# m kept in DRAM as two parts, split where it is made, and six early pairs of the second feed-forward, each split ahead of the puts

## The chip, the cores and the metric

One core of a Trainium2 chip runs the whole kernel. The metric is the device time of one execution in microseconds. Before the change it is 2270.53 us, the median of three runs (2268.02 to 2271.82). The engines are named as the profile names them: PE (TensorE, matmuls), PEld (its weight loads), DVE (VectorE), ACT (ScalarE), POOL (GpSimd) and SP (the sync engine, which issues loads).

## The reference

One layer of a trunk on 1024 tokens of width 1024: a half-step feed-forward, a token mixing of two branches (retention and neighbourhood attention), and a second half-step feed-forward, each with RMS norms before and after. What matters here is the end of the mixing and the start of the second feed-forward:

```python
merged = jax.nn.sigmoid(g_ret) * y_ret + jax.nn.sigmoid(g_na) * y_na
return merged @ w_out
...
x = x + _rms_norm(m, mix_post_norm[l])
h = _swiglu(_rms_norm(x, ffn2_pre_norm[l]), ffn2_w_in[l], ffn2_w_out[l])
x = x + 0.5 * _rms_norm(h, ffn2_post_norm[l])
```

## The kernel before

Every matmul operand is a float32 that is **split** into two parts of a rounded type, h and l with h + l the value: `split` (L56) casts h on ACT and subtracts on DVE to get l. `mm3` (L86) then makes one product of three matmuls, h·h, h·l and l·h. `piece` (L75) splits 512 columns of a weight into `wh` and `wl`, of which there are eight buffers each.

**Making m** (L1453 to L1479). `merged`, here called m, is made feature by feature: eight tiles of 128 features x 1024 tokens in the groups 0 to 2, 3 to 5 and 6 to 7. For each tile 48 matmuls make `y_ret`; DVE multiplies the two banks by the gate (`sr`, loaded into the tile `m`, L1477) and adds the other branch (tile `z`, L1478), and POOL's queue stores the tile to DRAM (L1479). The tiles `m` and `z` have four buffers each.

**Mix-out** (`out_proj`, L137, called at L1508). `merged @ w_out` runs over token blocks of 128 in three groups: blocks 0 to 2, 3 to 5, 6 and 7. In a group the loop goes over the eight k, the feature tiles of m; in the last three k the blocks are finished one after another. `stream` (L842) brings the left side: SP loads the k's slice of m (`graw`, two buffers), and `split` makes `gh` and `gl` (three buffers each). `wload` (L1490) brings the weights, which stay for all groups. When a block is finished, `Ep` (L210) makes its norm and residual, stores x2 and starts the norm for the feed-forward; its last step, a closure in the list `left`, turns the block by eight transposes on PE (`flip`, L122) and hands it to `Winograd.put` (L264).

**The puts.** The second feed-forward's first matmul is done by a scheme with seven products in place of eight (Winograd). Its left operands are a11 and a12 from blocks 0 to 3, and a22, s1, s2, s3 and s4, for which blocks 4 to 7 are needed too. The put of a block from 4 to 7 is eleven operations of DVE and seven of ACT.

**Pairs** (L409). One pair is the gate tile and the up tile of 128 features. `run` (L494) makes its products: a11, s2, a12, s3, s1, a22, s4, 12 matmuls each. Products a11 and a12 don't need blocks 4 to 7, so `lead` (L454) makes them early, between mix-out and the last puts: before the change for four pairs. Three pairs stay in PSUM (pairs 0, 1, 2, "held"), and one (pair 3, "saved") is made first and copied to SBUF, in pieces of 256 columns in buffers of `gh` and `gl`, through `save` (L1512). The list `between` holds the closures that mix-out left over (the flips of blocks 6 and 7, then the last steps of their puts); one is taken after each early pair. After that, `ffn_in` (L539) runs all 22 pairs; the first four are "begun" and lack two products. In `run`, `t2` is the operand of product s2, and L510, L511, L521 and L530 are the four subtractions on weights; `LeftFactors` (L562) splits and stores what a pair has made for the next matmul.

The order on each engine is the scheduler's; each engine executes its own queue in order. PE's work is cut into stages whose windows the prediction names: making m, mix-out, the lead (mix-out's end to the first product s2), the begun pairs, and the rest.

Of the kernel before, what the change touches and what calls it, by code (L numbers as in the profile page):

```python
# [1 line left out]

# [8 lines left out]
F32 = mybir.dt.float32  # L11
F32R = mybir.dt.float32r
# [6 lines left out]
P = 128  # L19
D = 1024  # L20
S = 1024
KT = D // P
TT = S // P
DFF = 2816
FT = DFF // P
# [13 lines left out]
class Core:  # L39
# [16 lines left out]
    def split(self, h, l, src, scale=None, eng=None):  # L56

        nc = self.nc
        hf = h.bitcast(F32)
        if scale is None:  # L60
            self.done = [nc.scalar.copy(h, src).ins,  # L61
                         (eng or nc.vector).tensor_tensor(l, src, hf, ALU.subtract).ins]  # L62
        else:
            nc.scalar.activation(h, src, AF.Copy, scale=scale)
            nc.vector.scalar_tensor_tensor(l, src, scale, hf, op0=ALU.mult, op1=ALU.subtract)
# [336 lines left out]
def xslice(xop):  # L402
    def f(k, h):
        s = slice(h * 512, (h + 1) * 512)
        return xop[0][k // 4][:, k % 4, s], xop[1][k // 4][:, k % 4, s]
    return f


class Pairs:  # L409
# [41 lines left out]
                               k == 0, k == 3)  # L451
                    yield

    def lead(self, save=None, between=(), on_pool=(), abreast=1, extra=0):  # L454


        n = self.held + self.saved
        tiles = [i for i in (*range(self.held, n), *range(self.held), *range(n, n + extra)) if i not in self.begun]
        while tiles:
            group, tiles, abreast = tiles[:abreast], tiles[abreast:], 1  # L460
            for i in group:
                if i not in self.fetched:
                    self.fetch(i)
            g = [self.fetched.pop(i) for i in group]
            eng = self.c.nc.gpsimd if group[0] in on_pool else None
            tag = ("ps", 6) if group[0] < n else ("pt", 2)
            ps = [self.products("a11", [self.ready.pop(i, w[:, :512]) for i, w in zip(group, g)], eng, tag),
                  self.products("a12", [w[:, 512:] for w in g], eng, tag)]
            if between:
                f = between.pop(0)()  # L470
                if f is not None:
                    between.append(f)
            for i, *pair in zip(group, *ps):
                if self.held <= i < n:
                    sb = [save(), save()]
                    for a, b in zip(sb, pair):
                        for p, s in self.pieces(a):
                            self.c.nc.scalar.copy(p, b[:, s])
                    pair = sb
                self.begun[i] = pair  # L480
# [358 lines left out]
    return flips  # L839


def stream(c, pool, src):  # L842

    def lhs(k, toks):
        n = len(toks) * P
        p0 = toks[0] * P
        raw = pool.tile([P, 384], F32, tag="graw", name="graw", bufs=2)
        h = pool.tile([P, 384], F32R, tag="gh", name="gh", bufs=3)
        l = pool.tile([P, 384], F32R, tag="gl", name="gl", bufs=3)
        c.nc.sync.dma_start(raw[:, :n], src(k)[:, p0:p0 + n])  # L850
        c.split(h[:, :n], l[:, :n], raw[:, :n])
        return {t: (h[:, j * P:(j + 1) * P], l[:, j * P:(j + 1) * P]) for j, t in enumerate(toks)}
    return lhs

# [344 lines left out]
def trunk_layer(ctx: ExitStack, tc, x, xt, g1a, w1i, w1o, g1b, gma, wmt, wnv, wrv, logits, dtab, rope, bias,  # L1199
# [7 lines left out]
    c = Core(tc, const, wpool, psum, dram)  # L1207
# [3 lines left out]
    def dt(name, shape):  # L1211
        return dram.tile(shape, F32, name=name)

    gl = [{n: dram.tile([FT // 2, P, 1024], F32, name=f"g{i}{n}") for n in Winograd.NAMES} for i in range(2)]
    x1, x2 = dt("x1", [S, D]), dt("x2", [S, D])
    d = {
        "a21": dt("a21", [P, 4, 512]),
        "nq": dt("nq", [NHP, P, S]), "nk": dt("nk", [NHP, P, S]), "nv": dt("nv", [16, 64, 512]), "nvg": dt("nvg", [4, 4, P, 512]),
        "no": dt("no", [NHP, P, S]), "rq": dt("rq", [RH, P, S]), "rk": dt("rk", [RH, P, S]),
        "rv": dt("rv", [TT, P, D]), "rg": dt("rg", [8, P, S]), "ry": dt("ry", [8, P, S]),  # L1220
        "sr": dt("sr", [8, P, S]), "sn": dt("sn", [8, P, S]), "z": dt("z", [8, P, S]), "m": dt("m", [8, P, S]),
    }

    def rows(a):
        return lambda t: a[t * P:(t + 1) * P, :]

    right, left = ExitStack(), ExitStack()

    def pool(stack, name, side="left"):
        return stack.enter_context(tc.tile_pool(name=name, bufs=1, side=side, reuse_waits="tile"))  # L1230
# [3 lines left out]
    early = pool(right, "early", "right")  # L1234
    wx = Winograd(c, apool, early, None, order=("s4", "a22", "s3", "a12", "s1", "s2", "a11"))
    g0 = pool(left, "gl10")
    with tc.tile_pool(name="fin1", bufs=1, reuse_waits="tile") as fp:
        def lead():
            return early.tile([P, 512], F32, tag="lead", name="lead", bufs=6)
# [5 lines left out]
        fin = Pairs(c, wx, [(w1i[i], w1i[FT + i]) for i in LeftFactors.order], 3, 3)  # L1245
# [4 lines left out]
        for _ in steps:  # L1250
# [8 lines left out]
    wx = Winograd(c, (x0pool, x1pool, spool), None, (4, 4, 2, 8, 8, 8, 8), d["a21"])  # L1259
# [5 lines left out]
    q = [p.tile([P, 4, 512], F32, tag="x", name="q", bufs=n) for p, n in ((ep, 2), (ep, 2), (spool, 8), (spool, 8))]  # L1265
    ahead = {}
    fo = Epilogue(c, ep, g1b, gma, rows(x), rows(x1), wx.put)
    rest = ffn_out(c, [[b11, b12], [b21, b22]], q, Blocks(c, (g0, *[g1] * 6)), w1o, gl[0], fo, tail,
                   {n: (lambda j=j: ahead.update({j: c.load_w(wnv[j])})) for j, n in enumerate((65, 66))})
# [63 lines left out]
    with tc.tile_pool(name="pa", bufs=1, reuse_waits="tile") as pa:  # L1333
# [12 lines left out]
        for i, (_, _, f, g, fn) in enumerate(jobs):  # L1346
# [18 lines left out]
            if i == 2:  # L1365
                x1pool = pool(x1_stack, "x1b", "right")
                a21[:] = [x1pool.tile([P, 4, 512], F32R, name=f"a21{q}") for q in "hl"]
                for k in range(2):
                    raw = c.raw(d["a21"][:, 2 * k:2 * k + 2].rearrange("p k t -> p (k t)"))
# [78 lines left out]
    gs = pool(g_stack, "gs2", "right")  # L1448
    ro = pool(y_stack, "ro")
    for k in range(KT):  # L1450
        raw = c.raw(d["ry"][k])
        c.split(yop[0][k // 4][:, k % 4], yop[1][k // 4][:, k % 4], raw)
    for i0 in (0, 3, 6):  # L1453
        tiles = range(i0, min(i0 + 3, 8))
        m, z, w, banks = {}, {}, {}, {}
        for i in tiles:
            w[i] = wr.pop(i) if i in wr else c.load_w(wro[i])
            banks[i] = [c.bank() for _ in range(2)]
            for q, name, src in ((m, "m", "sr"), (z, "z", "z")):
                q[i] = ro.tile([P, S], F32, tag=name, name=name, bufs=4)  # L1460
                nc.sync.dma_start(q[i], d[src][i])

        def one(i, k):
            ks = slice((k % 4) * P, (k % 4 + 1) * P)
            for h in range(2):
                c.mm3(banks[i][h], [p[:, ks] for p in w[i][k // 4]], xslice(yop)(k, h), k == 0, k == KT - 1)


        for k in range(KT if i0 == 0 else 0):
            for i in tiles:  # L1470
                one(i, k)
        for i in tiles:
            for k in range(KT if i0 > 0 else 0):
                one(i, k)
            for h in range(2):
                hs = slice(h * 512, (h + 1) * 512)
                nc.vector.tensor_tensor(m[i][:, hs], banks[i][h], m[i][:, hs], ALU.mult)  # L1477
                nc.vector.tensor_tensor(m[i][:, hs], m[i][:, hs], z[i][:, hs], ALU.add)  # L1478
            c.store(d["m"][i], m[i])  # L1479
    y_stack.close()  # L1480
    m_stack.close()

    a_stack, wm_stack = ExitStack(), ExitStack()
    apool = pool(a_stack, "a2", "right")
    wm = pool(wm_stack, "wm", "right")
    cmb = pool(left, "cmb2")
    wx = Winograd(c, apool, cmb, None, order=("s1", "s3", "a12", "s2", "a11"))
    held = {}

# [15 lines left out]

    with tc.tile_pool(name="ep2", bufs=1, reuse_waits="tile") as ep:
        ks = tuple(range(KT))
        rest = c.out_proj(KT, stream(c, gs, lambda k: d["m"][k]), wload,  # L1508
                          Ep(c, ep, gmb, g2a, False, rows(x1), rows(x2), wx.put), (ks, ks, ks[4:] + ks[:4]), lags={4: 11})
        fin = Pairs(c, wx, [(w2i[i], w2i[FT + i]) for i in LeftFactors.order], 3, 1)  # L1510

        def save():  # L1512
            return [gs.tile([P, 384], F32, tag=n, name=n, bufs=3)[:, :256] for n in ("gh", "gl")]

        rest.insert(0, lambda: None)
        fin.lead(save, rest)
        for f in rest:
            f()

# [7 lines left out]
    w = [w2.tile([P, 4, 512], F32, name=f"w{i}") for i in range(12)]  # L1527
    tiles = [[[w[n] for n in m] for m in q] for q in (((11, 10, 9), (8, 7, 6)), ((2, 1, 0), (5, 4, 3)))]
    with tc.tile_pool(name="out2", bufs=1, reuse_waits="tile") as op:
        q = [op.tile([P, 4, 512], F32, tag="q", name="q", bufs=4) for _ in range(4)]  # L1530
# [82 lines left out]
```

## Time and profile before

| what | value |
|---|---|
| median of 3 runs | 2270.53 us |
| the profiled execution, whole | 2266.95 us |
| its span, first to last instruction | 2265.2 us |
| mean granted clock of PE | 0.992 |
| moved by DMA | 439.91 MB, mean 194 GB/s |
| mix-out's first and last split of m's slices | 1484.1 and 1610.4 us |

The profile's page gives shares over the whole span. The stages are read from windows (busy time of each engine in a stretch), the causes from the wait views (who waited for whom), and single steps from the timeline, where a row is the start, the duration, the engine, line, operation, output and inputs, the count, and in brackets the idle time before it and what ended it. Matmul rows overlap: a matmul of 512 columns is shown as 0.39 us, and the next starts 0.227 us after it.

### The profile page before, as it was taken

To read this page: it belongs to the slowest core of one execution; us is meant where nothing else is said; L and a number is where in the kernel's file an instruction comes from. 1 tells how busy PE (TensorE), PEld (TensorE's weight loads), DVE (VectorE), ACT (ScalarE), POOL (GpSimd) and SP (SyncE) were. 2 spreads that over 40 slices of the span, in tenths; PEclk is the share of its full clock that TensorE was granted. 3 is DMA by queue.
4 is the path that set the end of the run, shared out by engine and by line. 5 is a ranking of instruction groups with operands and counts; after the bars stand their busy time and mean duration, and the time that the engine had idled before them with its cause. 6 is when DMAs were issued, how large, how long until landed. Compare 5 with 4: busy or idle time off the path is not lost. (4 is left out here: it accounts for less than half of the span.)

```text
span 2265.2 us, 30039 instructions
## 1 busy us (share of the span) xinstructions
PE 2204.2 (97%) x10232; PEld 1830.1 (81%) x10232; DVE 1641.4 (72%) x2928; ACT 984.5 (43%) x2054; POOL 575.8 (25%) x747
## 2 busy tenths in 40 slices
PE   6899999999998999999999999999999999999998
PEld 5688888888786887878888888887778888888886
DVE  7898878765558757769885678544998787876444
ACT  5444434332344322248885676323644343433232
POOL 1121212168521122311101222101112121215942
PEclk9999999999999999999999999999999999999999
DMA  6354434597545554557655466764345444449765
GB/s 251 134 181 150 177 130 170 187 387 294 199 174 174 180 173 134 145 181 241 217 173 174 151 230 233 259 232 144 117 156 188 149 161 147 154 157 378 283 225 180
DMA packets 150345, 439.91 MB, mean 194 GB/s; under 512 B 19056, under 2 KB 46832, under 8 KB 148080
## 3 DMA queue, kind: packets, MB, share of 16 engines
q1 hardware_dynamic: 108912, 305.84, 39.4%
q0 software_dynamic: 41280, 132.15, 16.2%
q8 instruction: 81, 1.33, 0.2%
q14 instruction: 72, 0.59, 0.1%
HBM read 297.41 MB, written 144.70 MB: 195 GB/s over the span
## 5 line engine op out<-in xcount | busy, mean ns | idle before, releaser
L62 DVE TENSOR_TENSOR wl<-wraw,wh 128x512 fp32r<-128x512 f32 x472 | 317.1, 689 | 66.3 <-ACT wh L61 66.0
L61 ACT CAST wh<-wraw 128x512 fp32r<-128x512 f32 x476 | 274.2, 618 | 169.2 <-PE ps L89 69.2
L88 PE MATMUL ps<-wh,g 128*128 128x512 f32 x484 | 188.8, 390 | 0.0
L89 PE MATMUL ps<-wl,g 128*128 128x512 f32 x484 | 188.7, 390 | 0.0
L90 PE MATMUL ps<-wh,g 128*128 128x512 f32 x484 | 188.5, 390 | 0.0
L552 ACT ACTIVATE c<-c 128x512 f32<-128x512 f32 x88 | 55.5, 632 | 208.0 <-DVE c L517 107.6
L62 DVE TENSOR_TENSOR wl<-w,wh 128x512 fp32r<-128x512 f32 x77 | 77.9, 1031 | 86.3 <-ACT wh L61 86.1
L62 DVE TENSOR_TENSOR wl<-x,wh 128x512 fp32r<-128x512 f32 x77 | 78.4, 1035 | 78.3 <-ACT wh L61 77.1
L61 ACT CAST wh<-t 128x512 fp32r<-128x512 f32 x58 | 36.0, 621 | 195.0 <-DVE t L511 194.9
L88 PE MATMUL ps<-a11h,wh 128*128 128x512 f32 x276 | 111.5, 404 | 7.9 <-ACT wh L61 7.9
L90 PE MATMUL ps<-a11h,wl 128*128 128x512 f32 x276 | 109.7, 398 | 7.3 <-DVE wl L62 7.2
L90 PE MATMUL ps<-a12h,wl 128*128 128x512 f32 x276 | 108.7, 394 | 3.4 <-DVE wl L62 3.4
L88 PE MATMUL ps<-a12h,wh 128*128 128x512 f32 x276 | 109.7, 397 | 0.5 <-ACT wh L61 0.3
L89 PE MATMUL ps<-a11l,wh 128*128 128x512 f32 x276 | 109.8, 398 | 0.1
L90 PE MATMUL ps<-a22h,wl 128*128 128x512 f32 x280 | 109.3, 390 | 0.6 <-DVE wl L62 0.6
L88 PE MATMUL ps<-a22h,wh 128*128 128x512 f32 x280 | 109.8, 392 | 0.0
L89 PE MATMUL ps<-a22l,wh 128*128 128x512 f32 x280 | 109.2, 390 | 0.0
L89 PE MATMUL ps<-a12l,wh 128*128 128x512 f32 x276 | 108.2, 392 | 0.0
L89 PEld LDWEIGHTS ps<-wl,g 128*128 128x128 f32 x484 | 90.9, 188 | 19.1 <-DVE wl L62 0.5
L90 PEld LDWEIGHTS ps<-wh,g 128*128 128x128 f32 x484 | 90.9, 188 | 18.8
L88 PEld LDWEIGHTS ps<-wh,g 128*128 128x128 f32 x484 | 90.9, 188 | 18.7
L88 PE MATMUL ps<-s2h,wh 128*128 128x512 f32 x232 | 91.9, 396 | 6.6 <-ACT wh L61 6.5
(438 smaller groups left out, 6411.4 us busy)
## 6 DMA issues: line engine op xcount, KB each, us to landing
wraw<-in_dram SPq DMA_DIRECT2D x202, 512.0 KB, 4.5
g<-g0s SPq DMA_DIRECT2D x44, 512.0 KB, 4.2
g<-g1s SPq DMA_DIRECT2D x44, 512.0 KB, 4.9
g<-g0a SPq DMA_DIRECT2D x33, 512.0 KB, 3.3
g<-g1a SPq DMA_DIRECT2D x33, 512.0 KB, 4.5
g0s<-gth POOLq DMA_DIRECT2D x44, 256.0 KB, 4.7
g0s<-cmb POOLq DMA_DIRECT2D x44, 256.0 KB, 3.7
g1s<-gth POOLq DMA_DIRECT2D x44, 256.0 KB, 4.6
```

The costliest lines, as they stand in the source:

```text
L61: self.done = [nc.scalar.copy(h, src).ins, (eng or nc.vector).tensor_tensor(l, src, hf, ALU.subtract).ins]
L62: (eng or nc.vector).tensor_tensor(l, src, hf, ALU.subtract).ins]
L88: mm(ps, a[0], b[0], start=start, stop=False)
L89: mm(ps, a[0], b[1], start=False, stop=False)
L90: mm(ps, a[1], b[0], start=False, stop=stop)
L552: nc.scalar.activation(gate[j], gate[j], AF.Silu)
```

## The change

In making m, each tile is split there: ACT casts h into the tile `z`, DVE leaves l in the tile `m`, and both are stored, so the DRAM tensor m has two parts. `stream` then loads the two parts straight into the operands: two loads of a slice per k and no split. Its eight buffers of 128x512 are six in the pool `gs` and two in a new pool `gx`, the latter for every fourth k.

Six pairs are begun early instead of four: pairs 3, 4 and 5 are saved, each product as one copy of 512 columns in a buffer of the stream, then 0, 1 and 2 are held. After the products of an early pair, and before the closure from `between`, the weights of the next early pair are split (`split` in `lead`). `between` starts with a closure that does nothing, then block 6's flip, another that does nothing, block 7's flip, and so on; before, only one stood at the front.

```diff
-    def lead(self, save=None, between=(), on_pool=(), abreast=1, extra=0):
+    def lead(self, save=None, between=(), on_pool=(), abreast=1, extra=0, early=False):
+        def split(i):
+            if i not in self.fetched:
+                self.fetch(i)
+            w = self.fetched[i]
+            self.ready[i] = self.c.piece(w[:, :512])
+            self.fetched[i] = [None, self.c.piece(w[:, 512:])]
...
-            ps = [self.products("a11", [self.ready.pop(i, w[:, :512]) for i, w in zip(group, g)], eng, tag),
-                  self.products("a12", [w[:, 512:] for w in g], eng, tag)]
+            ps = [self.products("a11", [self.ready.pop(i) if i in self.ready else w[:, :512] for i, w in zip(group, g)],
+                                eng, tag),
+                  self.products("a12", [w[1] if isinstance(w, list) else w[:, 512:] for w in g], eng, tag)]
+            if early and tiles:
+                split(tiles[0])
             if between:
...
-def stream(c, pool, src):
+def stream(c, pools, src):
+    n0 = itertools.count()
     def lhs(k, toks):
...
-        raw = pool.tile([P, 384], F32, tag="graw", name="graw", bufs=2)
-        h = pool.tile([P, 384], F32R, tag="gh", name="gh", bufs=3)
-        l = pool.tile([P, 384], F32R, tag="gl", name="gl", bufs=3)
-        c.nc.sync.dma_start(raw[:, :n], src(k)[:, p0:p0 + n])
-        c.split(h[:, :n], l[:, :n], raw[:, :n])
+        last = next(n0) % 4 == 3
+        h, l = (pools[last].tile([P, 512], F32, tag="g", name="g", bufs=2 if last else 6) for _ in range(2))
+        for q, a in enumerate((h, l)):
+            c.nc.sync.dma_start(a[:, :n], src(k, q)[:, p0:p0 + n])
+        h, l = h.bitcast(F32R), l.bitcast(F32R)
...
-            c.store(d["m"][i], m[i])
+            c.split(z[i].bitcast(F32R), m[i].bitcast(F32R), m[i])
+            for q, a in enumerate((z[i], m[i])):
+                c.store(d["m"][i][q], a)
...
-        fin = Pairs(c, wx, [(w2i[i], w2i[FT + i]) for i in LeftFactors.order], 3, 1)
+        fin = Pairs(c, wx, [(w2i[i], w2i[FT + i]) for i in LeftFactors.order], 3, 3)
         def save():
-            return [gs.tile([P, 384], F32, tag=n, name=n, bufs=3)[:, :256] for n in ("gh", "gl")]
-        rest.insert(0, lambda: None)
-        fin.lead(save, rest)
+            return gs.tile([P, 512], F32, tag="g", name="g", bufs=6)
+        rest[1:1] = rest[:0] = [lambda: None]
+        fin.lead(save, rest, early=True)
```

What this does to the order of the engines shows at two places. The line numbers of the changed kernel are 1 to 12 higher.

The first place is DVE near the end of the lead, where block 7's put begins: `wl` is a split of an early pair's weight; `cmb`, `a22l` and `s1l` to `s4l` belong to the puts of blocks 6 and 7. Before, from the sum of block 7's L283 on:

```order
L283 TENSOR_TENSOR cmb<-cmb,a11l 128x512
L293 TENSOR_TENSOR cmb<-a12h,cmb 128x512
L62 TENSOR_TENSOR a22l<-pt,a22h 128x4x128
L294 TENSOR_TENSOR cmb<-cmb,a12l 128x512
L288 TENSOR_TENSOR cmb<-pt,cmb 128x512
L62 TENSOR_TENSOR s3l<-cmb,s3h 128x4x128
L62 TENSOR_TENSOR wl<-wraw,wh 128x512
L290 TENSOR_TENSOR cmb<-pt,cmb 128x512
L62 TENSOR_TENSOR s1l<-cmb,s1h 128x4x128
L62 TENSOR_TENSOR s4l<-cmb,s4h 128x4x128
L62 TENSOR_TENSOR s2l<-cmb,s2h 128x4x128
```

Now:

```order
L63 TENSOR_TENSOR wl<-wraw,wh 128x512
L63 TENSOR_TENSOR s2l<-cmb,s2h 128x4x128
L63 TENSOR_TENSOR wl<-wraw,wh 128x512
L294 TENSOR_TENSOR cmb<-a12h,cmb 128x512
L63 TENSOR_TENSOR wl<-wraw,wh 128x512
L295 TENSOR_TENSOR cmb<-cmb,a12l 128x512
L520 TENSOR_TENSOR wraw<-wraw 128x512
L283 TENSOR_TENSOR cmb<-a11h,cmb 128x512
L63 TENSOR_TENSOR a22l<-pt,a22h 128x4x128
L284 TENSOR_TENSOR cmb<-cmb,a11l 128x512
L289 TENSOR_TENSOR cmb<-pt,cmb 128x512
```

The last weight splits of the early pairs, before in the midst of block 7's put, now stand ahead of its first step (L283 in the changed kernel), among the steps of block 6's.

The second place is DVE in the begun pairs. `t_16351` is t2 of pair 3, the last that was begun before; L535 is the last add of pair 2. Before:

```order
L510 TENSOR_TENSOR wraw<-wraw 128x512
L517 TENSOR_TENSOR c_16344<-gh,gt 128x256
L532 TENSOR_TENSOR c_16199<-ps,c_16199 128x512
L511 TENSOR_TENSOR t_16351<-wraw 128x512
L517 TENSOR_TENSOR c_16344<-gl,gt 128x256
L554 TENSOR_TENSOR gt<-c_16199,gt 128x512
L62 TENSOR_TENSOR wl<-t_16351,wh 128x512
L535 TENSOR_TENSOR gt<-ps,gt 128x512
```

Now the last begun pair is pair 5, its t2 is `t_16667`, and L545 is the last add of pair 4 (L610 are splits of `LeftFactors`, L564 its gate times up):

```order
L542 TENSOR_TENSOR c_16515<-ps,c_16515 128x512
L610 TENSOR_TENSOR cmb<-cmb,gth 128x512
L520 TENSOR_TENSOR wraw<-wraw 128x512
L564 TENSOR_TENSOR gt<-c_16515,gt 128x512
L521 TENSOR_TENSOR t_16667<-wraw 128x512
L545 TENSOR_TENSOR gt<-ps,gt 128x512
L527 TENSOR_TENSOR c_16660<-g,gt 128x512
L564 TENSOR_TENSOR gt<-c_16514,gt 128x512
L63 TENSOR_TENSOR wl<-t_16667,wh 128x512
```

The split of t2 moved from ahead of the last add of the pair before it to behind that add. From the split of pair 3's t2 (`t_16406` in the changed kernel) to that of pair 5's, this one included, DVE has 47 operations.

More of the change, by code (lines that the diff above doesn't have):

```diff
@@ L1 @@
+import itertools
 from contextlib import ExitStack, nullcontext
@@ L1220, in trunk_layer @@
         "rv": dt("rv", [TT, P, D]), "rg": dt("rg", [8, P, S]), "ry": dt("ry", [8, P, S]),
-        "sr": dt("sr", [8, P, S]), "sn": dt("sn", [8, P, S]), "z": dt("z", [8, P, S]), "m": dt("m", [8, P, S]),
+        "sr": dt("sr", [8, P, S]), "sn": dt("sn", [8, P, S]), "z": dt("z", [8, P, S]), "m": dt("m", [8, 2, P, S]),
     }
@@ L1485, in trunk_layer @@
     wm = pool(wm_stack, "wm", "right")
-    cmb = pool(left, "cmb2")
+    cmb, gx = pool(left, "cmb2"), pool(left, "gx")
     wx = Winograd(c, apool, cmb, None, order=("s1", "s3", "a12", "s2", "a11"))
@@ L1507, in trunk_layer @@
         ks = tuple(range(KT))
-        rest = c.out_proj(KT, stream(c, gs, lambda k: d["m"][k]), wload,
+        rest = c.out_proj(KT, stream(c, (gs, gx), lambda k, q: d["m"][k][q]), wload,
                           Ep(c, ep, gmb, g2a, False, rows(x1), rows(x2), wx.put), (ks, ks, ks[4:] + ks[:4]), lags={4: 11})
-        fin = Pairs(c, wx, [(w2i[i], w2i[FT + i]) for i in LeftFactors.order], 3, 1)
+        fin = Pairs(c, wx, [(w2i[i], w2i[FT + i]) for i in LeftFactors.order], 3, 3)
         def save():
-            return [gs.tile([P, 384], F32, tag=n, name=n, bufs=3)[:, :256] for n in ("gh", "gl")]
-        rest.insert(0, lambda: None)
-        fin.lead(save, rest)
+            return gs.tile([P, 512], F32, tag="g", name="g", bufs=6)
+        rest[1:1] = rest[:0] = [lambda: None]
+        fin.lead(save, rest, early=True)
         for f in rest:
```

## The prediction

> **What bounds the kernel now.** First the page (engine totals), then the windows by stage. Columns of a window: length, busy us and instructions of PE, PEld, DVE, ACT and POOL, granted clock, DMA share, GB/s.
>
> ```profile
> PE 2204.2 (97%) x10232; PEld 1830.1 (81%) x10232; DVE 1641.4 (72%) x2928; ACT 984.5 (43%) x2054; POOL 575.8 (25%) x747
> ...
> 1433.00:1520.00 87.00, 87.00 (x385) 72.08 (x385) 40.35 (x58) 17.83 (x26) 5.40 (x10) 1.00 0.74 270
> 1520.00:1616.00 96.00, 94.50 (x436) 76.81 (x435) 58.79 (x107) 42.49 (x105) 11.06 (x19) 1.00 0.41 144
> 1616.00:1650.00 34.00, 28.31 (x122) 21.79 (x121) 32.64 (x57) 18.98 (x41) 4.61 (x6) 0.95 0.27 93
> 1650.00:1705.00 55.00, 54.89 (x242) 44.80 (x241) 52.93 (x89) 23.59 (x44) 8.65 (x16) 1.00 0.46 163
> 1705.00:2250.00 545.00, 545.00 (x2405) 451.34 (x2404) 381.89 (x570) 196.36 (x355) 185.96 (x218) 1.00 0.56 205
> ```
>
> TensorE is the bound, and from 1705 to 2250 it has no gap at all: whatever it gains or loses before comes out at the end one for one. The five rows are the stage that makes m, mix-out, the lead, the begun pairs, and the rest. TensorE idles 1.5 us in mix-out and 5.7 us in the lead, where VectorE is busy 32.64 of 34 us. The wait views of TensorE for these two stretches (us, times, longest) name the releasers:
>
> ```profile
> PE pt L127 <- DVE tmp L118: 0.5, 1, 0.5
> PE pt L127 <- DVE a12l L62: 0.4, 1, 0.4
> PE ps L90 <- DVE gl L62: 0.3, 1, 0.3
> PE ps L88 <- DVE tmp L225: 0.2, 1, 0.2
> ```
>
> ```profile
> PE ps L90 <- DVE wl L62: 4.8, 3, 3.4
> PE ps L88 <- ACT wh L61: 0.8, 1, 0.8
> ```
>
> All of it is VectorE and its partner ScalarE. The change leaves TensorE's matmuls as many as before and moves some, so the forecast is this idle time removed, less idle time that it adds.
>
> **Making m.** Eight splits of 128x1024 come in; the nearest rows are the same two operations on the same size, in this stage, on `ry`:
>
> ```profile
> L61 ACT CAST xy<-wraw x8: 1031/1048/1056, 1431.0 to 1446.5; 128x1024 fp32r<-128x1024 f32 x8
> L62 DVE TENSOR_TENSOR xy<-wraw,xy x8: 1214/1220/1226, 1432.9 to 1447.6; 128x1024 fp32r<-128x1024 f32 x8
> ```
>
> So 8 x 1.05 = 8.4 us of ScalarE and 8 x 1.22 = 9.8 us of VectorE, in 87 us of which they are busy 17.8 and 40.4; TensorE waits for neither. What this delays is behind it: `z` and `m` of tile i are now free only when both stores have landed, and tile i+4 loads into them. The DMA rows (KB each, median us to landing):
>
> ```profile
> z<-z SPq DMA_DIRECT2D x8, 512.0 KB, 7.8
> m<-m POOLq DMA_DIRECT2D x8, 512.0 KB, 4.9
> ...
> graw<-m SPq DMA_DIRECT2D x16, 192.0 KB, 3.3
> ```
>
> ```profile
> 1466.27 0.54 POOL L68 DMA_DIRECT2D m<-m  x1 [29.49 <-DVE m L1478]
> ```
>
> The second fence is GpSimd's first store of m in the timeline, at 1466.3. Now one cast comes ahead of it: the store of tile 0's `z` goes at about 1467.3, lands 4.9 later, and z of tile 4 is there 7.8 after that: 1480. VectorE needs it when tile 4's matmuls end, 240 matmuls of 0.227 us after the stage's start at 1434: 1488. I put **0**; the bounds are 0 and, if each landing took twice as long, 5 us. The added bytes are 4 MB out and 4 MB in; at the 270 GB/s of the first row that is 30 us of transfer laid into 183 us with DMA shares of 0.74 and 0.41.
>
> **Mix-out.** 24 splits go, on both engines:
>
> ```profile
> L61 ACT CAST gh<-graw x24: 397/514/516, 1484.1 to 1608.7; 128x384 fp32r<-128x384 f32 x16, 128x256 fp32r<-128x256 f32 x8
> L62 DVE TENSOR_TENSOR gl<-graw,gh x24: 415/551/559, 1484.7 to 1610.4; 128x384 fp32r<-128x384 f32 x16, 128x256 fp32r<-128x256 f32 x8
> ```
>
> That is 16 x 0.55 + 8 x 0.42 = 12.2 us of VectorE. They stood in front of the epilogues for which TensorE waited:
>
> ```profile
> 1559.12 0.56 DVE L62 TENSOR_TENSOR gl<-graw,gh 128x384 fp32r<-128x384 f32 x1 [0.98 <-ACT gh L61]
> ...
> 1560.22 1.41 DVE L118 SCALAR_TENSOR_TENSOR tmp<-epx,rstd,gpre 128x512 f32<-128x512 f32 x2
> ...
> 1601.02 0.39 PE L88 MATMUL ps<-wmh,gh 128*128 128x512 f32 x1
> 1601.75 0.51 PE L90 MATMUL ps<-wmh,gl 128*128 128x512 f32 x1 [0.34 <-DVE gl L62]
> ```
>
> VectorE sat 0.98 us for `gh` and then did `gl` ahead of L118; without them L118 is over 1 us earlier, more than the 0.5 us wait. A pause costs more than its idle time: 1601.02 to 1601.75 is 0.73 where 0.23 would do. The four waits cost about 3 us so counted. I take **-2.0** (bounds -3 and 0), as the wait for the bank that `a12l` frees may stay in part.
>
> The price is on the sync queue: each k takes two loads. A k-step of three blocks is 18 matmuls, 4.1 us, and a buffer pair is free about 6.8 us ahead of its use at the tightest (the eighth k of a group, in its last three). 3.3 us to landing, and some 0.4 more for the second issue, fit: **0**. Landings of twice that would stall each group once for about half a microsecond, so the bounds are 0 and 2 us.
>
> **The lead.** TensorE's rows (start, us):
>
> ```profile
> 1616.64 0.39 PE L88 MATMUL ps<-a11h,wh 128*128 128x512 f32 x1
> 1616.87 0.39 PE L89 MATMUL ps<-a11l,wh 128*128 128x512 f32 x1
> ...
> 1636.37 0.50 PE L90 MATMUL ps<-a11h,wl 128*128 128x512 f32 x1 [1.05 <-DVE wl L62]
> ...
> 1642.98 0.50 PE L90 MATMUL ps<-a12h,wl 128*128 128x512 f32 x1 [3.38 <-DVE wl L62]
> ...
> 1646.36 0.63 PE L90 MATMUL ps<-a12h,wl 128*128 128x512 f32 x1
> 1647.84 0.50 PE L88 MATMUL ps<-s2h,wh 128*128 128x512 f32 x1 [0.85 <-ACT wh L61]
> 1648.18 0.40 PE L89 MATMUL ps<-s2l,wh 128*128 128x512 f32 x1
> 1648.99 0.50 PE L90 MATMUL ps<-s2h,wl 128*128 128x512 f32 x1 [0.41 <-DVE wl L62]
> ```
>
> From 1616.64 to 1647.84 are 31.2 us for 96 matmuls (x 0.227 = 21.8) and 16 transposes (steps around them: 2.0 us); 7.4 are lost, and 0.8 more at the start of `s2`: **8.2 us**. One part is a slow clock: 0.63 instead of 0.39 us for eight matmuls after the long wait. Why the wait is there:
>
> ```profile
> 1617.33 0.21 DVE L220 TENSOR_SCALAR ss<-ss 128x1 f32<-128x1 f32 x1
> ...
> 1641.64 0.68 DVE L62 TENSOR_TENSOR s3l<-cmb,s3h 128x512 fp32r<-128x512 f32 x1
> 1642.24 0.69 DVE L62 TENSOR_TENSOR wl<-wraw,wh 128x512 fp32r<-128x512 f32 x1
> ...
> 1644.64 0.69 DVE L62 TENSOR_TENSOR s2l<-cmb,s2h 128x512 fp32r<-128x512 f32 x1
> ```
>
> The split of the last early pair stood between the steps of block 7's put. In the new order (first place above) it stands ahead of that put. And there are 144 matmuls: `s2` is reached at 1616.6 + 144 x 0.227 + 1.8 for two flips = 1651.1, in the old time. VectorE steps by 0.60 us (1641.64 to 1642.24). From block 6's epilogue (1617.33) to block 7's last first-hand split `s2l` (1644.64, done at 1645.2) it never waits for TensorE in this trace; in the new order this stretch has six operations more (three weight splits, three of the first pair), and one more to the split of the first pair's t2: 1645.2 + 7 x 0.60 = 1649.4, where TensorE wants it at the third matmul of `s2`, 1651.6. Block 7's first put step is then due 12 operations earlier, at 1642.2, and its transposes end at 1616.6 + 96 x 0.227 + 1.8 = 1640.2. So **-8.2**, with 2.2 us to spare. ScalarE gets some 5 us more (four casts, and six saves of whole banks where there were four of half ones) in a stretch where it is busy 19 of 34 us: 0.
>
> **The begun pairs.** A begun pair is five products, 60 matmuls, 13.6 us of TensorE; a full one has seven, 19.0 us. VectorE's share is 23.5 operations per pair on average (18 of its own, 11 per two pairs for the factors of the second product), 14.1 us. Already the fourth begun pair comes too late (VectorE's split of its t2, and TensorE's `s2`):
>
> ```profile
> 1689.51 0.69 DVE L62 TENSOR_TENSOR wl<-t,wh 128x512 fp32r<-128x512 f32 x1
> ```
>
> ```profile
> 1689.47 0.44 PE L88 MATMUL ps<-s2h,wh 128*128 128x512 f32 x1
> ...
> 1690.25 0.50 PE L90 MATMUL ps<-s2h,wl 128*128 128x512 f32 x1
> ```
>
> The third matmul of `s2`, due 0.45 us after the first, is 0.3 us late. Now two more begun pairs follow: the order has 47 VectorE operations after pair 3's t2 split up to pair 5's (second place above), 28.3 us, against 27.2 us of TensorE: 1.1 later; and the split now stands behind the last add of the pair before, which waits for that pair's last product: 0.6 more. Together **+2.0** at pair 5 (bounds 0 and 5: nothing if ScalarE's and VectorE's order leaves slack, twice as much if waits for a buffer's store fall in). The Trainium skill (TensorE: Matmul & The Clock Gate, "What's actually happening") lets the clock halve after an idle window of about 3.4 us; the trace agrees, with slow matmuls after 3.38 us idle and none after 1.05 or 0.85. By that rule 2 us stays without a slow clock, and a wait above 3.4 would cost some 1.4 us on top.
>
> **Sum.** 0 - 2.0 - 8.2 + 2.0 = -8.2 us. The profiled execution took 2266.95 us, so it would take 2258.7. The median of the runs is 3.6 above it, and I predict against the median: **2262.3**.
>
> **Rivals.** (1) The whole idle time goes, the begun pairs cost nothing: -11, 2259.5. For it: in the row 1650 to 1705 four begun pairs cost TensorE only 0.1 us of idle time. Against it: the count of 47 operations. (2) VectorE stays the bound in the lead or the pairs, waits move there, and only some 3 us are left: 2267.5. For it: 32.64 of 34 us busy. Against it: 12 us of work leave it just ahead. It decides once the put of block 7 starts over 2.2 us later than I count. (3) The change does not do what it says: TensorE reaches `s2` later but waits there as long as before, 2270.5. Against it: the long wait was for a weight split, not for the put. (4) Slower: the two loads of a k land one after the other. From the row that is 2 x 3.3 = 6.6 us per k-step against 4.1 in mix-out's first two groups: 16 x 2.5 = +40 us, less the gain: 2302; it decides from 4.1 us per pair of loads. Against it: in the stage before, the DMA share reaches 0.74 with 270 GB/s, and 512 KB in 4.9 or 7.8 us each would be 107 or 67 GB/s one after the other, so transfers overlap. The Trainium skill (DMA: Bandwidth & Descriptors, "Anatomy of one DMA") fits a transfer, though for the GpSimd path, as 2.0 us plus its bytes at 436 GB/s: two of 192 KB in a row would be, as an estimate, 2 x 2.45 = 4.9 us, and the loss 16 x 0.8 = 13 us. Here the trace differs: one such load took 3.3 us to landing from the sync queue.
>
> **Chances.** Forecast (-6 to -10) 0.60, (1) 0.10, (2) 0.15, (3) 0.08, (4) or any like it 0.07. Range: 2257 (all idle time gone, and the 2 us by which runs scatter) to 2270 (nearly nothing left). 0.2% is 4.5 us, about what a measurement of this kernel tells from no change: faster holds the forecast, (1) and half of (2), 0.77; same 0.16; slower 0.07.
>
> **What would show it.** In the changed profile: no wait of TensorE for `wl` between the end of mix-out and `s2`, and no slow clock there; `s2` some 34.5 us after the lead's first matmul; a TensorE wait of about 2 us for `wl` at the sixth pair's `s2`; mix-out's idle time under 0.7 us; no TensorE wait for a load of `m`. It would be wrong if VectorE reaches block 7's put after about 1644 in the old time, or if stream loads take over 6.8 us.

## The result, and the profile after

| | before | changed |
|---|---|---|
| median of 5 runs (range), us | 2268.02 (2267.3 to 2271.82) | 2259.97 (2256.05 to 2262.78) |
| span of the profiled execution, us | 2265.2 | 2258.2 |
| ratio of the runs | 1 | 0.9956, 95% interval 0.9944 to 0.9967 |

The changed kernel is faster, by 8.05 us between the medians; the ratio, taken over all runs, says 10 us, with an interval of 7.5 to 12.7. That is 0.4%, small but clear of the scatter. First the page's engine totals and the windows by stage, with the columns of the prediction's (length, busy us and instructions of PE, PEld, DVE, ACT, POOL, granted clock, DMA share, GB/s):

```profile
PE 2201.1 (97%) x10232; PEld 1828.9 (81%) x10232; DVE 1638.7 (73%) x2911; ACT 984.6 (44%) x2039; POOL 581.0 (26%) x755
```

```profile
1433.00:1520.00 87.00, 87.00 (x386) 72.05 (x385) 46.59 (x62) 22.57 (x29) 8.79 (x16) 1.00 0.84 312
1520.00:1614.00 94.00, 93.20 (x433) 76.69 (x432) 50.77 (x89) 34.51 (x85) 11.16 (x20) 1.00 0.59 199
1614.00:1650.00 36.00, 36.00 (x169) 29.96 (x168) 34.64 (x60) 23.98 (x49) 4.60 (x6) 1.00 0.29 102
1650.00:1733.00 83.00, 80.86 (x347) 65.78 (x346) 79.12 (x130) 33.47 (x60) 16.24 (x30) 0.98 0.52 184
1733.00:2240.00 507.00, 507.00 (x2238) 419.73 (x2237) 350.45 (x520) 182.54 (x329) 176.40 (x203) 1.00 0.58 208
```

Making m is full as before. Mix-out has 0.80 us of idle TensorE left, and the lead none at all. New is a hole of 2.1 us, with the clock at 0.98, in the begun pairs. From 1733 to 2240 there is no gap again, so all that was gained ahead of it reaches the end. The wait views of TensorE (us, times, longest), first mix-out, then the begun pairs; the lead's has no row.

```profile
PE ps L89 <- DVE tmp L226: 0.4, 1, 0.4
PE pt L128 <- DVE a11l L63: 0.3, 1, 0.3
```

```profile
PE ps L89 <- ACT wh L62: 1.2, 1, 1.2
PE ps L91 <- DVE wl L63: 1.0, 1, 1.0
```

The table counts TensorE's stages from first matmul to first matmul in the timelines (us). "Over" is the time above 0.227 us a matmul; the lead has 1.8 us on top for its flips, as in the prediction. The last stage is the first s2 and the 479 matmuls behind it, 108.6 us without a pause. The experiments stand in it too, told below.

| kernel | making m | mix-out | lead: early pairs, us, over | 480 matmuls, over |
|---|---|---|---|---|
| before | 87.04 | 95.64 | 4, 31.20, 7.6 | 1.4 |
| changed | 87.04 | 94.15 | 6, 34.46, 0.0 | 4.6 |
| e1_split_only | 87.05 | 94.06 | 4, 30.16, 6.6 | 3.5 |
| e2_six_only | 87.04 | 96.30 | 6, 35.97, 1.5 | 6.4 |
| e3_six_late | 87.04 | 94.06 | 6, 34.46, 0.0 | 3.0 |
| e4_pair6 | 87.04 | 94.15 | 6, 34.45, 0.0 | 0.9 |
| e5_tt_pool | 87.04 | 94.07 | 6, 34.45, 0.0 | 4.1 |
| e6_five | 87.04 | 94.13 | 5, 31.98, 3.0 | 2.9 |
| e7_double_load | 87.04 | 111.71 | 6, 34.45, 0.0 | 4.6 |
| e8_pair6_again | 87.04 | 94.05 | 6, 34.44, 0.0 | 1.3 |
| e9_double_aside | 87.04 | 94.14 | 6, 34.47, 0.0 | 4.6 |
| e10_same | 87.04 | 94.08 | 6, 34.45, 0.0 | 3.0 |

From before to changed that is 0 - 1.5 - 7.6 + 3.2 = -5.9 us. The stage that makes m also began 1.0 us earlier (1432.95 instead of 1433.96); this start lies between 1430.9 and 1440.6 in the twelve profiles and follows no edit. Together -6.9, and the spans differ by 7.0.

### The profile page after: what moved, and what is told of

It is laid out like the page before. It is cut to its first block, busy times and chain, and to the rows that moved or that the text cites. A ratio compares the mean times of both kernels' runs of the same rounds, so it can differ in the third digit from the quotient of the medians.

```text
span 2258.2 us, 30072 instructions
## 1 busy us (share of the span) xinstructions
PE 2201.1 (97%) x10232; PEld 1828.9 (81%) x10232; DVE 1638.7 (73%) x2911; ACT 984.6 (44%) x2039; POOL 581.0 (26%) x755
## 5 line engine op out<-in xcount | busy, mean ns | idle before, releaser
L89 PE MATMUL ps<-wh,g 128*128 128x512 f32 x548 | 214.2, 391 | 0.4 <-DVE tmp L226 0.4
L90 PE MATMUL ps<-wl,g 128*128 128x512 f32 x548 | 213.6, 390 | 0.0
L91 PE MATMUL ps<-wh,g 128*128 128x512 f32 x548 | 213.3, 389 | 0.0
L89 PEld LDWEIGHTS ps<-wh,g 128*128 128x128 f32 x548 | 102.9, 188 | 21.8 <-DVE tmp L226 0.7
L90 PEld LDWEIGHTS ps<-wl,g 128*128 128x128 f32 x548 | 102.9, 188 | 21.5 <-DVE wl L63 0.5
L91 PEld LDWEIGHTS ps<-wh,g 128*128 128x128 f32 x548 | 102.9, 188 | 21.4
```

The source lines that it names most:

```text
L89: mm(ps, a[0], b[0], start=start, stop=False)
L90: mm(ps, a[0], b[1], start=False, stop=False)
L91: mm(ps, a[1], b[0], start=False, stop=stop)
```

## The experiments

All are measured against the kernel before, run beside them on the same chip (three chips; the medians of the kernel before are 2268.16, 2269.57 and 2268.99 us), so ratios compare better than times. Diffs are against the changed kernel, unless said otherwise. A theory and a rival stand in each expectation.

**e1_split_only**: m in two parts, but four early pairs as before.

```diff
-        fin = Pairs(c, wx, [(w2i[i], w2i[FT + i]) for i in LeftFactors.order], 3, 3)
+        fin = Pairs(c, wx, [(w2i[i], w2i[FT + i]) for i in LeftFactors.order], 3, 1)
...
-        rest[1:1] = rest[:0] = [lambda: None]
-        fin.lead(save, rest, early=True)
+        rest.insert(0, lambda: None)
+        fin.lead(save, rest)
```

> Edit: the changed kernel with four early pairs in the old order; only m stays split in DRAM. Theory (two separate gains): mix-out loses about 1.5 us of TensorE's waits as in the changed kernel, the lead keeps its wait of 3 to 4 us for a weight split and its 8 us of loss, the last begun pair costs 0.4 us; time 1 to 2 us under the kernel before. Rival (the lead was late because VectorE came into it with a backlog from the 24 splits): the waits in the lead shrink to under 3 us in all and the time comes 5 to 7 us under the kernel before.

2267.15 us, ratio 0.9998 (0.9988 to 1.0007): no gain that can be told from the scatter. Mix-out has its 1.6 us, but the lead's wait is whole, in one piece at s2. TensorE's waits in the lead:

```profile
PE ps L89 <- ACT wh L62: 5.1, 1, 5.1
PE pt L128 <- ACT cmb L280: 0.7, 1, 0.7
PE ps L91 <- DVE wl L63: 0.5, 1, 0.5
```

So the 12 us of VectorE work that left mix-out don't free the lead by themselves, and the rival falls. That rests on the stages; the total also has the 2.1 us that the last stage lost, most of it (1.6) in eight slow matmuls behind the long wait.

**e2_six_only**: the kernel before with six early pairs split ahead of the puts, m in one part and split in mix-out (the saves go to other free buffers).

> Edit: the kernel before, with m as one part and 24 splits in mix-out, but six early pairs, each split ahead of the puts; the saves lie in pieces in the buffers of the stream. Theory: the lead has no wait over 0.3 us and s2 comes about 34.5 us after its first matmul, mix-out keeps its 1.5 us of idle time, pair 5 has the waits of the changed kernel (4 us of loss); time 4 to 5 us under the kernel before. Rival (the split in DRAM is what frees the lead): waits of 3 us or more remain in the lead, time within 2 us of the kernel before.

2263.81 us, ratio 0.9976 (0.9965 to 0.9988). Of the changed kernel's gain it has about half. One wait for a weight split is left in the lead, where the theory had none over 0.3 us:

```profile
PE ps L90 <- DVE wl L62: 1.1, 1, 1.1
```

Mix-out is 2.1 us longer than in the changed kernel, the lead 1.5, the begun pairs 1.8; the pauses at pair 5's s2 are 2.00 and 0.94 us, with slow matmuls behind them. With e1: the early pairs fill most of the lead's wait, and the split of m, worth nothing that shows alone, is worth some 4 us beside them (by the medians; part of it is the slow clock, told at the end).

**e3_six_late**: six early pairs, without the split ahead of the closures.

```diff
-        fin.lead(save, rest, early=True)
+        fin.lead(save, rest)
```

> Edit: the changed kernel, but the weights of an early pair are not split ahead of the puts; the six pairs and their places stay. Theory (the place of the splits matters by itself): VectorE does the last weight splits among the steps of block 7's put, and TensorE waits in the lead 2 to 5 us for them; time 2 to 5 us over the changed kernel. Rival (the two more pairs alone fill the wait): no wait over 0.5 us in the lead, time as the changed kernel's.

2259.83 us, ratio 0.996 (0.9949 to 0.9972), and no wait in the lead. The scheduler brings every engine's instructions into the same order as in the changed kernel, so the place of `split` in the code changed nothing, and the theory's claim for it fell. The run serves as a repeat of the changed kernel.

**e4_pair6**: six early pairs, but 0 to 4 and 6 instead of 0 to 5, so that one pair with all seven products stands ahead of the last begun one.

```diff
         tiles = [i for i in (*range(self.held, n), *range(self.held), *range(n, n + extra)) if i not in self.begun]
+        if early:
+            tiles[2] = 6
...
-            tag = ("ps", 6) if group[0] < n else ("pt", 2)
+            tag = ("ps", 6) if group[0] < n or early else ("pt", 2)
...
-                if self.held <= i < n:
+                if self.held <= i < n or early and i == 6:
```

> Edit: the changed kernel, but the early pairs are 0 to 4 and 6 in place of 5; nothing else. Theory (pair 5's s2 comes too early for VectorE, as five products are all that its predecessor gives it, and the work for the second product's factors falls there): a full pair 5 starts with a product that needs no subtraction, the waits at its s2 (1.2 and 1.0 us) and the slow matmuls after them go, and nothing as long takes their place; TensorE loses under 1 us between 1650 and 1800, time 3 to 4 us under the changed kernel. Rival (VectorE's backlog only moves on): a wait of 1.5 us or more at s2 of pair 6 or 7, time as the changed kernel's.

2257.12 us, ratio 0.9949 (0.9934 to 0.9965). The wait view of TensorE for the begun pairs (1650 to 1735), and the window that showed the hole:

```profile
PE ps L89 <- ACT wh L62: 0.3, 1, 0.3
```

```profile
1650.00:1733.00 83.00, 82.75 (x364) 67.67 (x363) 79.20 (x130) 36.04 (x64) 16.17 (x30) 1.00 0.50 181
```

VectorE is as busy as in the changed kernel (79.20 and 79.12 us), TensorE 1.9 us more: the work is the same, and a pair of 84 matmuls ahead of the last t2 gives it time. The pauses belong to too many short pairs in a row.

**e5_tt_pool**: the sums and differences of `LeftFactors` of the first six pairs on GpSimd.

```diff
-            return lambda: self.traced.append(c.nc.vector.tensor_tensor(*a).ins)
+            eng = c.nc.gpsimd if i < self.on_pool else c.nc.vector
+            return lambda: self.traced.append(eng.tensor_tensor(*a).ins)
...
-        tail = ffn_in(c, fin, fp, LeftFactors(c, cmb, fp, gl[1]))
+        tail = ffn_in(c, fin, fp, LeftFactors(c, cmb, fp, gl[1], 6))
```

> The changed kernel, but the sums and differences of LeftFactors (L589) of the first six pairs run on GpSimd instead of VectorE. Theory: in the begun pairs VectorE never pauses, and its count of operations alone sets when pair 5's t2 is split; four operations of 0.60 us fewer between pair 3's and pair 5's split bring that split 2.4 us earlier, so of its 2.5 us of lateness at most 0.5 is left, no slow matmuls follow, and the stretch of 480 matmuls after the first s2 falls from 113.2 to about 110: time about 2257. Rival: the order is held by a chain (the subtraction for t2 waits for what stands behind the last add of pair 4, or GpSimd's operations, about 1.5 us each, delay VectorE's splits behind them in its queue): then both waits at pair 5's s2 stay over 0.8 us each and the time stays at 2260 or rises.

2259.37 us, ratio 0.9962 (0.995 to 0.9975): no gain over the changed kernel. From pair 3's t2 split (1692.49) to pair 5's (1721.34) VectorE took 28.85 us, against 28.99 in the changed kernel. It had 40 operations there instead of 47, as three more (L527, L542, L564) fell outside; the 4.2 us so saved were given back at two places. At the first, an operation took 1.78 us instead of 0.68 (1696.76, 1.1 more). VectorE's and GpSimd's rows of the timeline at the second:

```profile
1713.62 0.69 DVE L612 TENSOR_TENSOR gt<-gt,gth 128x512 fp32r<-128x512 f32 x1 [2.08 <-POOL cmb L591]
1714.23 1.78 DVE L612 TENSOR_TENSOR cmb<-cmb,gth 128x512 fp32r<-128x512 f32 x1
```

```profile
1712.30 1.29 POOL L591 TENSOR_TENSOR cmb<-gt,cmb 128x512 f32<-128x512 f32 x1
...
1714.11 1.35 POOL L591 TENSOR_TENSOR cmb<-gt,cmb 128x512 f32<-128x512 f32 x1
```

A split that overwrites `gt` waited 2.08 us until GpSimd had read it, and the next one took 1.78 us instead of 0.69. TensorE still waits 0.96 us at pair 5's s2, and 0.97 us at its s3 in place of the 1.18 at s2. GpSimd's operations holding up VectorE is the rival's second half. So the run doesn't test whether the count of operations decides: VectorE was as late with fewer.

**e6_five**: five early pairs, two saved (`..., 3, 2)` in place of `..., 3, 3)`).

> The changed kernel with five early pairs (two saved) instead of six. Theory: the lead is a race of TensorE's 24 matmuls per early pair against VectorE's put of blocks 6 and 7. With 120 matmuls TensorE is at s2 120 x 0.227 + 1.8 = 29.0 us after the lead's start, its third matmul 29.45; VectorE's split of the first t2 ended 33.1 us after that start with six pairs, and three operations of 0.60 us fewer make 31.3: waits of about 1.9 us at the first s2 (and up to 1.6 us of slow matmuls), where four early pairs waited 5.1 and six none. At the last begun pair less than 1 us. Time 2259 to 2262. Rival: the wait is set by the put of block 7 and not by the count of early pairs: 5 us as with four, time 2265.

2261.54 us, ratio 0.9972 (0.9963 to 0.9982). TensorE's wait in the lead:

```profile
PE ps L89 <- ACT s2h L62: 2.8, 1, 2.8
```

The wait is 0.9 us longer than expected, since the last part of block 7's put (s2h) ended later than the weight split from which I had counted. By the lead's "over", four pairs (e1) lose 6.6 us and five 3.0: one pair more fills 3.6. That is what the race says, 24 matmuls (5.4 us) less three weight splits of VectorE (1.8 us); e1 also lacks the `split` and the second closure that does nothing, so the step isn't the pair's alone. From five to six the same step would leave 0.6 us to spare, but the changed kernel has 1.9 (told below): its s2h is ready 31.3 us after the lead's start, in e6 only after 31.9. ScalarE's row in the changed kernel, whose lead starts at 1614.14:

```profile
1644.80 0.62 ACT L62 CAST s2h<-cmb 128x512 fp32r<-128x512 f32 x1 [1.38 <-DVE cmb L291]
```

The order on VectorE moved as well: with five pairs three operations on the first pair's t2 (L521, L531 and its split) stand ahead of block 7's put, with six behind its start. So the count gives the direction and about the size, not each step.

The last begun pair has no wait, as expected, but pair 3's s2 waits 1.54 us, which I had not foreseen: ScalarE waited 2.42 us for a store of `gth` to land, VectorE 2.02 us for ScalarE, and the subtraction for t2 came late.

**e7_double_load**: each slice of m's parts loaded twice into its buffer.

```diff
-            c.nc.sync.dma_start(a[:, :n], src(k, q)[:, p0:p0 + n])
+            for _ in range(2):
+                c.nc.sync.dma_start(a[:, :n], src(k, q)[:, p0:p0 + n])
```

> The changed kernel, but each slice of the two parts of m is loaded twice into its buffer (64 loads of 192 KB more than needed count the same bytes twice: about 2 x 8 MB instead of 8 in mix-out). Theory: a buffer pair is free some 6.8 us ahead of its use at the tightest and the loads took 4.6 us to landing; at about twice that TensorE waits for a load of m once or twice per group, well under 1 us each: mix-out at most 2 us longer, time 2260 to 2262. Rival (the prediction's fourth): loads of one queue land one after the other, so every k-step of 4.1 us would wait for four loads: mix-out over 10 us longer, time over 2270.

2280.55 us, ratio 1.0049 (1.0031 to 1.0068); mix-out 17.6 us longer. TensorE's waits in mix-out, and the largest entry among the sync queue's own:

```profile
PE ps L89 <- DMA g<-m: 13.2, 7, 3.8
PE ps L91 <- DMA g<-m: 0.4, 1, 0.4
```

```profile
SPq L863 <- DMA g<-m: 32.3, 19, 4.6
```

The edit brought a wait that I hadn't meant: the second load into a place waits in the queue for the first to land, and everything behind it waits too. So it doesn't measure the margin; the next one comes nearer. (The edit adds 48 loads, not 64.)

**e9_double_aside**: as many further loads, with half the bytes, into the columns of the buffer that the slice leaves free.

```diff
             c.nc.sync.dma_start(a[:, :n], src(k, q)[:, p0:p0 + n])
+            c.nc.sync.dma_start(a[:, n:], src(k, q)[:, p0:p0 + 512 - n])
```

> The changed kernel with as many further loads of m's parts as it has (48), each of the tokens that come after the slice's first ones, into the columns of the same buffer that the slice leaves free (128 or 256 of 512), so that no load waits for another one: 96 loads in mix-out instead of 48, 12 MB in place of 8. Theory: with e7_double_load the loss of 17.6 us in mix-out came from the queue, which stood 32.3 us until a load had landed before the second into the same place could be issued; the prediction's margin (free 6.8 us ahead, 4.6 us to landing) leaves room for twice the loads: at most 2 us more in mix-out, time 2260 to 2262. Rival: loads from one queue hold each other up by their number and bytes; waits for a load of m on TensorE of 6 us or more in mix-out, time over 2266.

2261.1 us, ratio 0.9961 (0.9948 to 0.9973), mix-out 94.14. No load waited for another of m, and none of TensorE's waits names a load. The rows of the DMA view (KB, median us to landing) show loads as quick as in the changed kernel, where 192 KB took 4.6 too:

```profile
g<-m SPq DMA_DIRECT2D x32, 192.0 KB, 4.6
g<-m SPq DMA_DIRECT2D x32, 128.0 KB, 4.2
```

**e8_pair6_again**: e4_pair6 once more, beside e5 to e7.

> The same kernel as e4_pair6 (early pairs 0 to 4 and 6), beside the others on one chip, to settle its distance from the changed kernel and from the kernel with LeftFactors on GpSimd. Theory: no wait over 0.3 us at any s2 and no slow matmuls in the begun pairs, about 2257, ratio to before 0.995. Rival: its 2.7 us to the changed kernel were scatter, and it comes out at 2260.

2257.66 us, ratio 0.9957 (0.9943 to 0.997); waits of 0.29 and 0.26 us are the longest at an s2 or s3. In time the step from the changed kernel is within the scatter: ratios 0.9949 and 0.9957 here, 0.9956, 0.996 and 0.9957 for the changed kernel, e3 and e10. What is shown is the stage: 0.9 and 1.3 us over, in place of 3.0 to 4.6.

**e10_same**: the changed kernel as it is.

> The changed kernel as it is. It shows whether the ten slow matmuls behind the two pauses (1.18 and 0.97 us) at pair 5's s2 come back. Theory: the pauses are set by the order of VectorE and come back to 0.05 us; whether the clock drops behind them depends on when they fall, so slow matmuls come or not (the stretch of 480 matmuls after the first s2 is 111.6 or 113.2). Rival: the slow matmuls belong to the order itself and come each time, 113.2.

2258.76 us, ratio 0.9957 (0.9938 to 0.9976). The pauses came back to the hundredth, the slow matmuls didn't. First the changed kernel, then e10_same, TensorE's timeline at pair 5's s2:

```profile
1716.67 0.39 PE L91 MATMUL ps<-s4h,wl 128*128 128x512 f32 x1
1718.23 0.50 PE L89 MATMUL ps<-s2h,wh 128*128 128x512 f32 x1 [1.18 <-ACT wh L62]
1718.57 0.40 PE L90 MATMUL ps<-s2l,wh 128*128 128x512 f32 x1
1719.93 0.57 PE L91 MATMUL ps<-s2h,wl 128*128 128x512 f32 x1 [0.97 <-DVE wl L63]
1720.30 0.63 PE L89 MATMUL ps<-s2h,wh 128*128 128x512 f32 x1
1720.73 0.63 PE L90 MATMUL ps<-s2l,wh 128*128 128x512 f32 x1
```

```profile
1718.62 0.50 PE L89 MATMUL ps<-s2h,wh 128*128 128x512 f32 x1 [1.18 <-ACT wh L62]
1718.96 0.40 PE L90 MATMUL ps<-s2l,wh 128*128 128x512 f32 x1
1720.32 0.50 PE L91 MATMUL ps<-s2h,wl 128*128 128x512 f32 x1 [0.97 <-DVE wl L63]
1720.66 0.40 PE L89 MATMUL ps<-s2h,wh 128*128 128x512 f32 x1
```

In the first the matmuls step by 0.43 us until 1723.69, in the second by 0.23 at once.

## Why the prediction was right, and where a size was off

**Making m, 0:** right. It took 87.04 us in both kernels. The first store of a part, as foreseen, comes one cast later: 33.4 us after the stage's start instead of 32.3.

```profile
1466.35 0.55 POOL L69 DMA_DIRECT2D m<-z  x1 [30.86 <-ACT z L62]
```

```profile
m<-sr SPq DMA_DIRECT2D x8, 512.0 KB, 8.4
z<-z SPq DMA_DIRECT2D x8, 512.0 KB, 8.1
m<-z POOLq DMA_DIRECT2D x8, 512.0 KB, 6.5
m<-m POOLq DMA_DIRECT2D x8, 512.0 KB, 7.4
```

The stores landed 6.5 and 7.4 us after their issue, not 4.9, with the DMA share up from 0.74 to 0.84; the 8 us of slack took that.

**Mix-out, -2.0:** -1.5. The waits for L118 and for `gl` went; of the other two, one stayed at 0.3 us, and the wait for `tmp` came out at 0.4; together they cost some 1.0 with the steps beside them. The named sign, idle time under 0.7, was just missed (0.80).

**The loads, 0 (to 2):** right. A load of 192 KB lands 4.6 us after its issue, where 3.3 and some 0.4 were put, and e9 shows that as many loads again, with half the bytes, don't matter. The fourth rival fell, but e7 shows what would have made it true: a load that waits at the head of the queue.

**The lead, -8.2:** right in place and size. s2 comes 34.46 us after the lead's first matmul, forecast 34.5, with no wait and the clock at 1.00. The spare time was put at 2.2 us; VectorE and TensorE at s2:

```profile
1646.49 0.68 DVE L63 TENSOR_TENSOR wl<-t,wh 128x512 fp32r<-128x512 f32 x1
```

```profile
1648.60 0.39 PE L89 MATMUL ps<-s2h,wh 128*128 128x512 f32 x1
1648.82 0.39 PE L90 MATMUL ps<-s2l,wh 128*128 128x512 f32 x1
1649.05 0.39 PE L91 MATMUL ps<-s2h,wl 128*128 128x512 f32 x1
```

The split ends at 1647.17, the third matmul starts at 1649.05: 1.9 us, and the put's s2h, done at 1645.42, is 3.2 us ahead of its use. The reason given, that the splits now stand ahead of block 7's put, needs one correction: e3 shows that the scheduler puts them there without the new `split`. It leaves open whether the six pairs alone do that or the second closure that does nothing is needed too, as no run has one without the other.

**The begun pairs, +2.0:** right in place, mis-sized. The mechanism is as written: pair 5's t2 split came too late, after 47 operations. VectorE's splits of pair 3's and pair 5's t2, and TensorE's third matmul of pair 3's s2:

```profile
1690.20 0.68 DVE L63 TENSOR_TENSOR wl<-t,wh 128x512 fp32r<-128x512 f32 x1
...
1719.19 0.68 DVE L63 TENSOR_TENSOR wl<-t,wh 128x512 fp32r<-128x512 f32 x1
```

```profile
1690.94 0.51 PE L91 MATMUL ps<-s2h,wl 128*128 128x512 f32 x1
```

VectorE took 28.99 us, forecast 28.3 + 0.6 = 28.9. That these agree is luck: the 0.6 was put for the last add of pair 4 waiting for its product, and VectorE came to that add without waiting:

```profile
1717.39 0.68 DVE L545 TENSOR_TENSOR gt<-ps,gt 128x512 f32<-128x512 f32 x1
```

The 0.7 us over 28.3 are four short stalls between 1695 and 1709, steps of 0.72 to 0.81 us in place of 0.60. TensorE took less than the 27.2 us that I had put against it: in pair 3 four matmuls of s3 and s1 already stood ahead of that third one, which leaves 116 x 0.227 = 26.3. That makes 2.7 us; the third matmul came at 1719.93, where 1717.35 (0.68 behind the last of s4) was its time: 2.6 late. That was split in two pauses, 1.18 us for ScalarE's cast of t2 and 0.97 for VectorE's split. The second error is the sentence that 2 us stay without a slow clock: the slow matmuls behind the pauses cost some 1.6 us in three of the five records with these two pauses (changed, e7, e9) and nothing in the other two (e3, e10); the last section shows why. So the term was 2.5 or about 4.1.

**Sum:** -8.2 forecast, -8.05 between the medians, -7.0 between the spans. The stages alone give -5.9. Against the forecast the begun pairs miss about 2 us and mix-out 0.5, and the early start of the stage that makes m, which is no effect of the change, gives 1.0 back in the spans. So that the medians come within 0.2 us of the forecast is partly luck: the stages of the profiled runs give 2.3 us less than the forecast, the ratio of all runs some 2 us more. The time of 2262.3 us was missed by 2.3, as the median of the kernel before fell by 2.5 with two more runs. The first rival (all idle time gone) would need pairs as in e4; the second and third fell, since the lead has no wait.

## What to carry to other kernels

When the bound engine waits behind another engine's queue, count both queues through the stretch: work for the bound engine that costs the other less (5.4 against 1.8 us a pair) fills the wait by about the difference (3.6 us a pair by the count; one step measured 3.6, the next, with its spare time, 4.9). But borrowed work is missing later: look where the pieces from which it was taken stand in a row, and spread them (pair 6 instead of 5). Before work is moved to an idle engine, look at who waits for its result or its reads; in e5 a 2.08 us wait and two operations slowed by 1.1 us each took back all that the move should bring.

## What was not expected of the hardware

The clock can drop behind pauses far below 3.4 us, and in the same program it does or doesn't: two pauses of 1.18 and 0.97 us, with two matmuls between them, were followed by matmuls that step by 0.43 us for 3.4 us (1720.30 to 1723.69), or by none. The traces show what decides. In each of the twelve profiles all changes of the granted clock lie on a grid of 3.413 us, which falls elsewhere in each run. Two stretches of that grid at pair 5's s2, first the changed kernel, then e3_six_late (length, TensorE's busy us and instructions, granted clock, DMA share, GB/s):

```profile
1716.81:1720.22 3.41, 1.27 (x5) 1.00 1.11 400
1720.22:1723.63 3.41, 3.41 (x9) 0.50 0.61 204
```

```profile
1720.99:1724.40 3.41, 2.06 (x8) 1.00 1.03 416
1724.40:1727.81 3.41, 2.62 (x11) 1.00 0.89 279
```

In the changed kernel both pauses fall into one stretch: TensorE idles 2.14 us of it, and the next one has half the clock. In e3 a border of the grid lies in the second pause, so no stretch has more than 1.35 us of idle time, and the clock stays. The other three fit: 2.15 (e9) and 1.65 (e7), slow; 1.44 (e10), not. In e2 the pause of 2.00 us alone, whole in one stretch, was enough. Over the twelve profiles, up to 2245 us, the 57 stretches behind which the clock dropped had 1.56 us of idle time or more, and of some 7500 behind which it stayed at full none had over 1.84. So about half a stretch is enough, and where the grid falls decides whether pauses of this size cost 1.6 us more; the same program got both (changed and e10). What decides between 1.56 and 1.84 stays open.

The Trainium skill (TensorE: Matmul & The Clock Gate, "What's actually happening") says that the gate watches a free-running window of some 3.4 us and halves the clock after an idle one. The traces agree on the window and differ on the idle time, of which about half a window was enough here; the prediction had read the page as a threshold for one pause.

In e5 a VectorE operation with two operands in SBUF that met a GpSimd operation took 1.78 us, three times between 1650 and 1740, instead of 0.68; the one quoted ended 0.55 us after GpSimd's own end (1714.11 + 1.35), as if it had waited for that. None of VectorE's additions and subtractions of that size there took over 1 us in the other eleven profiles. Whether it waited was not tested by itself.
